# Column chunks of two thirds of the tokens moved beside the GLA stage, in a two-layer hybrid trunk

## The chip, the cores and the metric

The kernel runs on one core of one Trainium2 chip. The metric is the device time of one execution in microseconds. Before the change it is 2963.45 us, the median of three runs (2956.27 to 2968.64).

## The reference

The reference computes two layers over 256 context tokens and 2048 latent tokens of width 1024. Cut to what matters:

```python
def hybrid_layer(x, ctx, ...):
    h_l = rms_norm(x, norm_w) * (1.0 + scale_l) + shift_l      # adaLN; the same for ctx with its own scale and shift
    pl = split_proj(h_l @ w_in)                                # 3104 columns: a_*, b_*, c_*, d_*
    a_l, a_c = gla_mixer(pl, pc, ...)      # A: gated linear attention, both directions, in chunks
    b_l = fourier_mix(pl['b_v'], fnet_w)   # B: 2-D FFT over tokens and channels, then a matrix
    c_l, c_c = swa_mixer(pl, pc, ...)      # C: windowed attention, +-128 tokens and the context, RoPE, sink
    d_l, d_c = na_mixer(pl, pc, ...)       # D: neighbourhood attention on a 64-wide grid, 8 x 16, with bias
    y_l = concat([a_l * silu(pl['a_g']), b_l * silu(pl['b_g']),
                  c_l * silu(pl['c_g']), d_l * silu(pl['d_g'])]) @ w_out
    x = x + gate_l * y_l                   # the context likewise, in the first layer only
```

All of it is float32. The projections are done in three passes (high times high, high times low, low times high parts), so each product of a 256-token sub-block with a chunk of 256 columns is 2 × 8 × 3 = 48 matmuls of 128x128 by 128x256.

## The kernel before

**Tiling.** The tokens are nine sub-blocks of 256 (sub-block 0 is the context), in three groups: T1 = 0, 1, 2; T2 = 3, 4, 5; T3 = 6, 7, 8. The 3104 input columns are twelve chunks of 256 and one of 32: av, aqk, lr (for the GLA), bv (FNet), ckv, cq (window attention), dk, dv, dq (neighbourhood attention) and four gates ag, bg, cg, dg. `project` (line 277) does one chunk for one sub-block: its 48 matmuls (lines 220 to 222) and its eviction. A gate's eviction is a tanh on ACT (line 292), a product on DVE (line 293) and a store of 256 KB. cq, ckv, dq and dk pass `normrope` (line 367), a chain over ACT, DVE and POOL, then two or four transposes and stores. The weights of a chunk are loaded by `load_w` (line 204) in four pieces of 256 KB, each split into a high part (ACT, line 212) and a low part (line 213, by turns DVE and POOL). There are two buffers for high and low parts, three for raw ones.

**h.** `prep_h` (line 244) normalises a sub-block, applies the adaLN scale and shift and leaves a high and a low part (`hh`, `hl`, three buffers each, shared with `prep_mix` of the output projection). For T1 and T2 it also stores h to DRAM (line 261). `reload_h` (line 264) brings it back later, with one cast on ACT and one subtraction on DVE or POOL per half.

**Stages of one layer** (`trunk`, line 198). For T1 and for T2: `first_chunks` (prep_h, then av, lr, aqk); `mix_a`, whose GLA has bv, ckv, dk, dv (in T2 also dq) between its heads and its main part `gla_fast` (line 399). For T3: `first_chunks`, `mix_a`, and then bv, ckv, dk, dv. Then a guard on the GLA's range, `gla_bwd` (line 646), `fnet` (line 689), cq and dq of T3. Then `attention`: 144 items in layer 0 (64 of neighbourhood attention, 72 of window attention and 8 context rows), 128 in layer 1, in a software pipeline (line 876). Between its items stand the rest of the projections: the gates of T3, then h of T1 reloaded, cq, dq and the gates of T1, h of T2 reloaded, cq and the gates of T2, and the output projections `out_proj` (line 1088). An item is the scores on PE (line 830), one custom DVE step that adds the bias or mask and finds the minimum (line 836, two records each: the step and a read of its accumulator), exp on ACT (line 844), transposes on PE (line 862), and, for two items at a time, the product with v (line 922). The scores have one PSUM buffer. The bias of the neighbourhood items is loaded to one buffer for each of a pair's two items (line 1012). Four items of window attention make one block of 128 tokens; 16 neighbourhood items make one row group, `rg`.

**adaLN.** `ada` (line 114) computes shifts, scales and gates by products on DVE (line 167) with weights loaded in pieces of 256 KB. Part 0 of layer 1 (shift and scale, needed by layer 1's first `prep_h`) is in layer 0's T2; part 1 (the gate) of each layer is in its own T1.

**Order.** The Python text gives each instruction a priority, earlier ones first (blocks under `high_priority` go ahead). A planner replays the program on a model of the engines and sends to each engine's queue the first instruction that is ready there, provided its buffers are free. On the chip each queue runs in the order so written. Nearly all DMAs are issued on SP's queue.

## Time and profile before

| | |
|---|---|
| median of three runs | 2963.45 us |
| the profiled execution | 2951.03 us |
| its span | 2949.1 us |
| PE busy | 92% of the span |
| mean granted clock of PE | 0.959 |
| DVE, ACT, POOL busy | 55%, 36%, 28% |
| DMA | 458 MB, 155 GB/s in the mean |

The span runs from the first to the last instruction of the program. Stages by time: layer 0's GLA to about 600 us, gla_bwd and FNet to 770, attention to 1450; layer 1 begins at about 1480, its gla_bwd at about 2100, its attention at 2260, and it ends with output projections. A busy PE is not PE at its peak: the trace models the ends of matmuls, so the distance between starts tells the pace. The granted clock is 1.00 at 2.4 GHz and 0.50 at 1.2 GHz; a mean between them tells what share of the stretch was spent at each.

### The profile page before, as it was taken

The numbers are of one execution on the slowest core, as the hardware profiler recorded it, in microseconds if no ns is written. First come the engines' busy times: TensorE is split into PE (matmuls) and PEld (weight loads), VectorE is DVE, ScalarE is ACT, GpSimd is POOL, SyncE is SP. The second block draws the span as 40 slices with busy tenths as digits, with TensorE's granted clock in tenths as the row PEclk, the third lists the DMA queues.
The fourth block names the chain that finished last, engine by engine and source line by source line (L and its number), as shares of the span: only waits on it lengthen the run. The fifth ranks groups of instructions, "written<-read, shape, count | busy, mean of one in ns | idle before, by whom it ended". The sixth has DMA issues, their size and how long they took to land. (4 is left out here: it accounts for less than half of the span.)

```text
span 2949.1 us, 55777 instructions
## 1 busy us (share of the span) xinstructions
PE 2718.3 (92%) x21206; PEld 2410.2 (82%) x21206; DVE 1609.3 (55%) x3741; ACT 1070.9 (36%) x2344; POOL 837.3 (28%) x922
## 2 busy tenths in 40 slices
PE   5989988988999999999959889999879999999998
PEld 5889878976888778887859889889768888878788
DVE  7554775557355454645484553464483646455543
ACT  3333323322344343344224323334232444444432
POOL 3233222234132121312133332332351313121222
PEclk9999988999999999999979999989999999999999
DMA  8635544245565274554464664333465654456545
GB/s 273 194 108 163 169 136 126 84 145 166 162 192 167 81 215 129 158 157 124 147 193 134 196 185 144 93 111 104 119 190 162 199 164 135 146 163 190 161 149 180
DMA packets 476681, 458.00 MB, mean 155 GB/s; under 512 B 54763, under 2 KB 355565, under 8 KB 476013
## 3 DMA queue, kind: packets, MB, share of 16 engines
q1 hardware_dynamic: 472782, 440.66, 48.9%
q0 software_dynamic: 3616, 13.64, 1.9%
q8 instruction: 170, 2.79, 0.4%
q14 instruction: 113, 0.93, 0.1%
HBM read 339.56 MB, written 114.60 MB: 154 GB/s over the span
## 5 line engine op out<-in xcount | busy, mean ns | idle before, releaser
L220 PE MATMUL ps<-whi,hh 128*128 128x256 f32 x1968 | 586.4, 298 | 34.7 <-ACT hh L258 17.2
L222 PE MATMUL ps<-whi,hl 128*128 128x256 f32 x1968 | 582.0, 296 | 10.2 <-DVE hl L259 10.2
L221 PE MATMUL ps<-wlo,hh 128*128 128x256 f32 x1968 | 580.8, 295 | 6.4 <-PEq L639 6.4
L213 POOL TENSOR_TENSOR wlo<-wraw,whi 128x512 fp32r<-128x512 f32 x208 | 280.8, 1350 | 775.7 <-ACT whi L212 735.1
L220 PEld LDWEIGHTS ps<-whi,hh 128*128 128x128 f32 x1968 | 391.9, 199 | 46.4 <-ACT hh L258 19.0
L220 PE MATMUL ps<-hh,whi 128*128 128x256 f32 x1376 | 402.5, 292 | 5.3 <-ACT ev L311 2.3
L222 PEld LDWEIGHTS ps<-whi,hl 128*128 128x128 f32 x1968 | 391.3, 199 | 18.5 <-DVE hl L259 13.9
L221 PE MATMUL ps<-hl,whi 128*128 128x256 f32 x1376 | 403.3, 293 | 0.0
L222 PE MATMUL ps<-hh,wlo 128*128 128x256 f32 x1376 | 402.4, 292 | 0.0
L221 PEld LDWEIGHTS ps<-wlo,hh 128*128 128x128 f32 x1968 | 392.4, 199 | 11.0 <-issue 8.8
L212 ACT CAST whi<-wraw 128x512 fp32r<-128x512 f32 x416 | 242.3, 620 | 378.5 <-DMA wraw<-w_in 206.9
L844 ACT ACTIVATE S<-S,am 128x641 f32<-128x641 f32 (+5 forms) x272 | 226.1, 831 | 339.1 <-DVE am L836 324.5
L220 PE MATMUL pso<-mh,whi 128*128 128x256 f32 x1088 | 316.7, 291 | 5.3 <-DVE xo L1107 2.9
L222 PE MATMUL pso<-mh,wlo 128*128 128x256 f32 x1088 | 316.2, 291 | 2.3 <-POOL wlo L213 1.8
L221 PE MATMUL pso<-ml,whi 128*128 128x256 f32 x1088 | 315.1, 290 | 0.0
L213 DVE TENSOR_TENSOR wlo<-wraw,whi 128x512 fp32r<-128x512 f32 x208 | 187.9, 907 | 170.9 <-ACT whi L212 163.4
L220 PEld LDWEIGHTS ps<-hh,whi 128*128 128x128 f32 x1376 | 265.9, 193 | 15.2 <-issue 7.9
L222 PEld LDWEIGHTS ps<-hh,wlo 128*128 128x128 f32 x1376 | 265.8, 193 | 15.1 <-issue 14.8
L221 PEld LDWEIGHTS ps<-hl,whi 128*128 128x128 f32 x1376 | 266.0, 193 | 11.4 <-issue 11.0
L830 PE MATMUL pse<-kst,q 64*128 64x256 f32 (+2 forms) x1184 | 246.6, 457 | 13.6 <-DVE am L836 12.5
L191 POOL TENSOR_TENSOR rs<-ms,mhalf 128x8 f32<-128x8 f32 (+2 forms) x140 | 171.3, 1226 | 297.5 <-DVE ms L189 288.6
L862 PE MATMUL ppt<-idn,S 128*128 128x128 f32 x1360 | 243.6, 284 | 10.4 <-DVE pt L872 5.2
(203 smaller groups left out, 4866.4 us busy)
## 6 DMA issues: line engine op xcount, KB each, us to landing
wraw<-w_in SPq DMA_DIRECT2D x288, 256.0 KB
wraw<-w_out SPq DMA_DIRECT2D x128, 256.0 KB
adaw<-ada_w SPq DMA_DIRECT2D x82, 256.0 KB
scr_g<-ev SPq DMA_DIRECT2D x68, 256.0 KB
g<-scr_g SPq DMA_DIRECT2D x34, 512.0 KB
y<-scr_y SPq DMA_DIRECT2D x34, 512.0 KB
bias<-nbias SPq DMA_DIRECT2D x48, 256.0 KB
scr_h<-x SPq DMA_DIRECT2D x22, 512.0 KB
```

The source lines that it names most:

```text
L191: nc.gpsimd.tensor_tensor(out=rs, in0=ms, in1=self.mhalf.to_broadcast([128, n]), op=ALU.pow)
L212: nc.scalar.copy(hi[:, k], raw)
L213: (nc.gpsimd if i % 4 else nc.vector).tensor_tensor(out=lo[:, k], in0=raw, in1=hi[:, k], op=ALU.subtract)
L220: nc.tensor.matmul(out, ah(k), bh(k), start=(k == 0), stop=False)
L221: nc.tensor.matmul(out, ah(k), bl(k), start=False, stop=False)
L222: nc.tensor.matmul(out, al(k), bh(k), start=False, stop=(k == KB - 1))
L830: nc.tensor.matmul(p[:, lo:hi], q[r], k, start=True, stop=True, tile_position=(64 * o, 0))
L844: nc.scalar.activation(out=S[:, 0:w], in_=S[:, 0:w], func=AF.Exp, scale=-1.0, bias=m[:, 0:1], accum_out=m[:, 1:2])
L862: nc.tensor.transpose(p[:, i], S[:, (c0 + i) * 128:(c0 + i + 1) * 128], self.idn)
```

## The change

T1 and T2 get all their columns in `mix_a`: bv, ckv, dk, dv, cq, dq and the four gates, between the GLA's heads and its main part. T3 gets cq, dq and all gates in one call after `fnet`, ahead of the attention. The attention has no projections between its items but `out_proj`, and these are all of the kind that is issued behind an item. h is neither stored nor reloaded; `reload_h` goes. In layer 0, `out_proj` of T1 stands ahead of the last window blocks 4 to 9, where it stood behind them and behind the gates of T2. Part 0 of layer 1's adaLN moves from layer 0's T2 to its T3.

```diff
-    def prep_h(self, L, s, save, xs=None):
+    def prep_h(self, L, s, xs=None):
...
-            if save:
-                nc.sync.dma_start(self.sh[s][:, :, c], x)
-    def reload_h(self, s):
...
-                    run, nop = lambda f=ph[1]: f(), lambda *r: None
-                    items.append((None, run, nop) if ph[0] == "before" else (None, nop, lambda r, x, f=ph[1]: x == 2 and f()))
+                    items.append((None, lambda: None, lambda r, x, f=ph[1]: x == 2 and f()))
...
-            self.mix_a(L, T1, (0, [1]) if L == 0 else (1, [1]), lambda: self.chunks(L, T1, kv, h))
+            qs = ["dq", "cq"]
+
+            def rest(subs, h):
+
+                self.chunks(L, subs, kv + qs + gates[:2], h)
+                self.chunks(L, subs, gates[2:], h)
+            self.mix_a(L, T1, (L, [1]), lambda: rest(T1, h))
...
             h = self.first_chunks(L, T2, first)
-            self.mix_a(L, T2, (1, [0]) if L == 0 else None, lambda: self.chunks(L, T2, kv + ["dq"], h))
-            h = self.first_chunks(L, T3, first, False)
-            self.mix_a(L, T3)
+            self.mix_a(L, T2, None, lambda: rest(T2, h))
+            h = self.first_chunks(L, T3, first)
+            self.mix_a(L, T3, (1, [0]) if L == 0 else None)
             self.chunks(L, T3, kv, h)
-            ws = {nm: self.chunk_w(L, nm) for nm in ("cq", "dq")}
+            ws = {nm: self.chunk_w(L, nm) for nm in qs}
...
-            self.chunks(L, T3, ["cq", "dq"], h, ws)
-            hs = {}
-
-            def redo(subs, names):
-                with self.tc.high_priority():
-                    hs[subs[-1]] = {s: self.reload_h(s) for s in subs}
-                self.chunks(L, subs, names, hs[subs[-1]])
-            hs[8] = h
-            b, f = (lambda f, *a: ("before", lambda: f(*a))), (lambda f, *a: ("after", lambda: f(*a)))
-            gate = lambda subs: b(lambda: self.chunks(L, subs, gates, hs[subs[-1]]))
-            ctx = ([-2, -1], None) if L == 0 else ([], )
+            self.chunks(L, T3, qs + gates, h, ws)
+            f = lambda subs: ("after", lambda: self.out_proj(L, subs))
             T1 = lat(T1)
-            ph = [3, 2, [10, 11, 12, 13, 14, 15], gate(T3), b(redo, T1, ["cq", "dq"]), 0, ctx[0] + [0, 1, 2, 3], *ctx[1:], gate(T1)]
             if L == 0:
-                ph += [b(self.out_proj, L, T3), b(redo, T2, ["cq"]), 1, [4, 5, 6, 7, 8, 9], gate(T2), f(self.out_proj, L, T1)]
+                self.attention(L, 3, 2, [10, 11, 12, 13, 14, 15], 0, f(T3), [-2, -1, 0, 1, 2, 3], None, 1, f(T1), [4, 5, 6, 7, 8, 9])
             else:
-                ph += [b(redo, T2, ["cq"]), 1, [4, 5], [6, 7], [8, 9], gate(T2), b(self.out_proj, L, T3), f(self.out_proj, L, T1),
-                       f(self.out_proj, L, [3, 4]), f(self.out_proj, L, [5])]
-            self.attention(L, *ph)
+                self.attention(L, 3, 2, [10, 11, 12, 13, 14, 15], 0, f(T3), [0, 1, 2, 3], 1, [4, 5], [6, 7], [8, 9], f(T1), f([3, 4]), f([5]))
```

A number in the list of an attention is a row group of neighbourhood attention (16 items), a list of numbers is window blocks (4 items each), `None` is the context's rows, `f(...)` an output projection.

## Rows read from the trace of the kernel before

**Rows 1.** The page, part 1: busy us, share of the span, instructions.

```profile
PE 2718.3 (92%) x21206; PEld 2410.2 (82%) x21206; DVE 1609.3 (55%) x3741; ACT 1070.9 (36%) x2344; POOL 837.3 (28%) x922
```

**Rows 2.** Windows by stage: start:end length, each engine's busy us, clock, DMA share, GB/s.

```profile
50.00:100.00 50.00, 38.86 (x296) 37.73 (x297) 29.84 (x72) 16.37 (x27) 14.50 (x16) 1.00 0.45 133
100.00:300.00 200.00, 184.97 (x1384) 174.72 (x1382) 110.34 (x261) 72.40 (x156) 62.48 (x54) 0.94 0.51 161
300.00:500.00 200.00, 173.96 (x1186) 159.33 (x1185) 138.56 (x341) 64.78 (x141) 56.08 (x49) 0.85 0.46 141
500.00:600.00 100.00, 99.50 (x776) 92.55 (x775) 45.64 (x116) 42.37 (x105) 31.33 (x25) 1.00 0.32 108
600.00:770.00 170.00, 144.43 (x923) 127.12 (x922) 102.46 (x257) 42.56 (x93) 65.68 (x60) 0.93 0.52 154
770.00:1450.00 680.00, 663.51 (x5603) 555.13 (x5603) 355.62 (x848) 276.91 (x639) 153.99 (x234) 0.99 0.51 151
1450.00:1550.00 100.00, 67.67 (x485) 65.50 (x484) 70.91 (x158) 21.56 (x31) 29.32 (x28) 0.80 0.65 201
1550.00:1750.00 200.00, 186.97 (x1439) 178.86 (x1437) 96.02 (x179) 72.77 (x147) 68.75 (x54) 0.96 0.54 169
1750.00:1950.00 200.00, 180.06 (x1314) 168.18 (x1312) 96.35 (x212) 71.96 (x152) 64.06 (x59) 0.91 0.38 118
2100.00:2260.00 160.00, 132.41 (x849) 115.99 (x850) 99.39 (x246) 38.39 (x86) 60.43 (x52) 0.93 0.53 159
2260.00:2850.00 590.00, 580.29 (x4962) 479.82 (x4961) 322.62 (x753) 256.53 (x587) 144.61 (x220) 0.99 0.57 166
```

**Rows 3.** PE's waits in 300:500: total us, times, longest.

```profile
PE pk L430 <- DVE A L422: 7.8, 2, 4.3
...
PE ps L220 <- DVE nsq L376: 5.4, 2, 4.9
```

**Rows 4.** Timeline of PE in the second attention: start, us, instruction.

```profile
2403.54 0.28 PE L220 MATMUL ps<-hh,whi 128*128 128x256 f32 x1
2403.66 0.28 PE L221 MATMUL ps<-hl,whi 128*128 128x256 f32 x1
```

**Rows 5.** Groups of instructions by line: count | busy us, mean ns | idle before.

```profile
L273 POOL TENSOR_TENSOR hl<-x,hh 128x1024 fp32r<-128x1024 f32 x11 | 28.0, 2543 | 42.8 <-ACT hh L272 38.1 <-PE ppt L862 4.7
...
L213 DVE TENSOR_TENSOR wlo<-wraw,whi 128x512 fp32r<-128x512 f32 x208 | 187.9, 907 | 170.9 <-ACT whi L212 163.4 <-DVEq L639 6.2 <-DMA wck<-wck 0.3
...
L293 DVE SCALAR_TENSOR_TENSOR ev<-ev,ps 128x512 f32<-128x512 f32 x68 | 46.4, 683 | 43.5 <-ACT ev L292 43.3
```

**Rows 6.** Windows of line 292 (ACT, two), then of line 836 (DVE, two).

```profile
600.00:770.00 170.00, 3.58 (x6) 0.93 0.52 154
770.00:836.00 66.00, 3.54 (x6) 0.97 0.75 206
...
770.00:836.00 66.00, 10.78 (x26) 0.97 0.75 206
2300.00:2600.00 300.00, 60.02 (x138) 1.00 0.53 155
```

**Rows 7.** Windows of line 167 on DVE, 300:500.

```profile
300.00:500.00 200.00, 48.48 (x128) 0.85 0.46 141
```

**Rows 8.** Window of line 220 on PE; lines 221 and 222 count the same.

```profile
770.00:1450.00 680.00, 271.81 (x933) 0.99 0.51 151
```

**Rows 9.** Timeline of DVE, two window items in a row.

```profile
2815.01 0.86 DVE L836 CUSTOM_DVE_ANT_0 S<-pse,cmask,sink 128x640 f32<-128x640 f32 x1
...
2817.23 0.87 DVE L836 CUSTOM_DVE_ANT_0 S<-pse,cmask,sink 128x640 f32<-128x640 f32 x1
```

**Rows 10.** Timeline of SP's queue, a bias load.

```profile
1253.77 0.54 SPq L1012 DMA_DIRECT2D bias<-nbias  x1
```

**Rows 11.** Timeline of DVE, two pairs of neighbourhood items.

```profile
1251.66 0.95 DVE L836 CUSTOM_DVE_ANT_0 S<-pse,bias 128x768 f32<-128x768 f32 x1
...
1259.89 0.96 DVE L836 CUSTOM_DVE_ANT_0 S<-pse,bias 128x768 f32<-128x768 f32 x1 [1.11 <-DMA bias<-nbias]
```

More of the change, by code (lines that the diff above doesn't have):

```diff
@@ L259, in prep_h @@
             nc.vector.tensor_tensor(out=hl[:, :, c], in0=x, in1=hh[:, :, c], op=ALU.subtract)
-            if save:
-                nc.sync.dma_start(self.sh[s][:, :, c], x)
-        return hh, hl
-    def reload_h(self, s):
-        nc = self.nc
-        hh = self.hp.tile([128, KB, SUB], F32R, tag="hh", name="hh2")
-        hl = self.hp.tile([128, KB, SUB], F32R, tag="hl", name="hl2")
-        for t in range(2):
-            c = slice(t * 128, t * 128 + 128)
-            x = self.xp.tile([128, KB, 128], F32, tag="xa", name="x2", bufs=3)
-            nc.sync.dma_start(x, self.sh[s][:, :, c])
-            nc.scalar.copy(hh[:, :, c], x)
-            (nc.gpsimd if t else nc.vector).tensor_tensor(out=hl[:, :, c], in0=x, in1=hh[:, :, c], op=ALU.subtract)
         return hh, hl
@@ L1119, in scratch @@
             self.xdst[L] = [None] + [a["out"][s] for s in range(NSUB - 1)]
-        self.sh = sc("h", [128, KB, SUB])
         self.skq, self.sbv, self.sav = (sc(n, [128, 2, SUB]) for n in ("kq", "bv", "av"))
@@ L1155, in order, with first_chunks @@
                 + [(nm, s) for g in (subs[:n], subs[n:]) for nm in (c, d) for s in g])
-    def first_chunks(self, L, subs, names, save=True, xs={}):
+    def first_chunks(self, L, subs, names, xs={}):
         h = {}
@@ L1161, in first_chunks @@
             with self.tc.high_priority():
-                h[s] = self.prep_h(L, s, save and not (L == 1 and s == 0), xs.get(s))
+                h[s] = self.prep_h(L, s, xs.get(s))
             for nm in names:
```

## The prediction

> **What bounds the kernel now.** I first read the page's busy shares [rows 1]: PE (TensorE's matmuls) is busy 92% of the span, DVE 55%, so PE is the engine to follow, and only time in which PE stands or runs at the lower clock can be won. Then the windows by stage [rows 2]. For each stretch I add two losses: the idle time of PE, and (1 − granted clock) × length. A fall from 2.4 to 1.2 GHz shows as a mean below 1.00 and doubles PE's work while it lasts. For 300:500 that is 26.0 us idle + 0.15 × 200 = 30 us, so 56 us. In the same way: 27 us in 100:300, 0.5 in 500:600, 37 in 600:770, 23 in 770:1450 (the first attention, 680 us long), 52 in 1450:1550 (between the layers), 21 and 38 in 1550:1750 and 1750:1950, 39 in 2100:2260, 16 in 2260:2850 (the second attention). So the attention stretches, which hold nearly half of the time, lose 39 us together, and the GLA and FNet stretches with the layers' border lose some 270.
>
> Why does PE stand in the GLA stretches? The waits of 300:500 [rows 3] say: for DVE's A and for a projection's normalisation on DVE. These are chains of small steps at moments when no other matmuls are at hand. In the attention stretches there are always projections to fill with. One projection of one sub-block (256 tokens) by one column chunk is 48 matmuls, one every 0.12 us where PE is dense [rows 4], so 5.8 us.
>
> **Part by part.** The number of matmuls does not change; they move.
>
> *h kept out of DRAM.* 22 stores and 22 loads go, with 22 casts on ACT and 22 subtractions on DVE and POOL (28.0 us on POOL's eleven) [rows 5]. These stood beside an attention in which PE lost almost nothing, and no matmul wait among [rows 3] is for them. I take 0; at most it is a few microseconds in the two attentions.
>
> *The move.* Per layer, cq, dq and four gates of T1 (18 projections; 12 in layer 1, where sub-block 0 is skipped) and cq and four gates of T2 (15) go from the attention into the GLA stretches: 33 × 5.8 = 190 us and 27 × 5.8 = 155 us of PE time. The 12 gates of T3 go ahead of the attention as well, but by 770 six of them have already been evicted, and six more by 836 [rows 6]: the planner already pulls them forward, and they still move little. Each gate brings a DVE step of 0.68 us, each chunk two DVE splits of 0.91 us [rows 5], two POOL splits, four ACT casts, and four loads and a store on SP's queue. For layer 0's T1 and T2 that is 24 × 0.68 + 11 chunks × 1.8 = 36 us of DVE, and nine normalised q projections at no more than the 5.8 us of their own matmuls, 52 us. DVE has 151 us free in 100:500 [rows 2], and the stretch grows by about as much as is moved in. So these hide; without that cover PE would wait for PSUM in the way that [rows 3] shows for nsq (5.4 us there).
>
> What it wins in T1 and T2 of layer 0 (27 + 56 us): waits where filler was missing go, waits where PE's in-order queue has reached a step that DVE has not finished stay. Of 300:500 I keep the two waits for A (7.8) and as my choice 12 us for the next T's first chunk and the clock: 20 left, 36 won. Of 100:300 I keep 12 and win 15. Bounds: 0 and 83.
>
> In layer 1, 59 us in 1550:1950: by the same share (51 of 83, 61%) 36; I take 27, since out_proj already fills part of T1. Bounds 0 and 59. In the FNet stretches (37 and 39) the chain over DVE is long (DVE is busy 102 of 170 us) and only the gates that were not there already come in: 9 won in each; bounds 0 and 37.
>
> *The adaLN part.* 128 records of line 167 on DVE (64 products, 48.5 us) stand in 300:500 [rows 7], beside T2's GLA; they move to 500:600, where DVE is busy 45.6 of 100 us [rows 2]. That makes 94 of 100, so DVE nearly becomes T3's bound there; its 32 loads go along on SP. PE's projections of T3 cover most of it. I charge 8 us; bounds 0 and 30. The gain on the side of T2 is in the 36 above. What would be late next is gla_bwd, which follows the guard.
>
> *The border between the layers.* out_proj of T1 now stands ahead of the last 24 window items of layer 0 instead of behind everything. The first x of layer 1 is then ready while those items run, and prep_h no longer runs alone. Of 52 us I take 30 as won. Bounds: 0 and 45.
>
> *The attentions without filler.* This is the price. Paced with filler, 138 records of line 836 (two per item, so 69 items) take 300 us [rows 6]: 4.35 us per item. PE's own share of an item: in 770:1450 PE is busy 663.5 us [rows 2]; of these 3 × 933 filling matmuls [rows 8] at 0.12 take 336, and 327.5 over 144 items leaves 2.3 us. How fast an item goes bare is not shown over any length. Single pairs show it: two window items 2.22 us apart [rows 9]. For neighbourhood items the bias tile has one buffer. Its load is issued only after its reader ended, at 1253.77 [rows 10], and the first item of the next pair starts at 1259.89 instead, held by the DMA, 8.23 us after the first of the pair before [rows 11]. So a neighbourhood item costs between 2.3 (PE) and 4.1 us; three of four pairs change the bias. I take 3.3 us for these, which is near the middle, and 2.5 us for window items, near their row. Bare are: in layer 0 items 13 (13 are done by 836 [rows 6]) to 59, when T3's out_proj can fill, and 14 more between T3's out_proj running out and T1's becoming ready; in layer 1, taken alike, some 44. That is together 104 items: 42 neighbourhood × 1.0 + 62 window × 0.2 = 54 us, and 6 us of lower clock: 60. Bounds: 0 and 4.35 − 2.3, times 104: 213.
>
> Sum: −15 − 36 + 8 − 9 − 30 − 27 − 9 + 60 = **−58 us**. The profiled execution took 2951.0 us by the clock (span 2949.1); the median shown is 12 us above that. 2951 − 58 + 12 = **2905 us**.
>
> **Rivals.**
> *The bare attention keeps its pace* (slower). If its items stay at 4.35 us, because the planned order of queues and loads holds them and not the filler, the price is 213 instead of 60: 2905 + 153 = 3058. For it: the pace is the same in stretches with different fillers, and bias loads already hold single items. Against it: 2.22 us [rows 9]. It decides from 118 of savings / 104 items, so from 3.4 us per bare item.
>
> *PE's clock falls in the bare attention* (slower). PE's 2.3 us become 4.6: 104 × 2.3 = 239 instead of 60, so 3084. Against it: in 50:100 PE is busy only 38.9 of 50 us, with gaps, and the clock is 1.00 [rows 2]. For it: 300:500 with PE busy 87% has 0.85. With filler the attention's clock was 0.99; no long bare stretch exists. The Trainium skill (TensorE: Matmul & The Clock Gate, "Why this matters for your kernels") warns that pauses between bursts of matmuls put the clock back to half. By that rule the bias waits of bare items would bring this rival about; the trace agrees so far as its falls stand in stretches with idle time.
>
> *The GLA waits stay.* If nearly all are in-order waits for DVE, filler behind the waiting instruction cannot pass. Then only the border's 30 are won against 60 + 8: 2963 + 38 = 3001. For it: the waits in [rows 3] name DVE. Against it: 500:600, with GLA and projections at hand, loses 0.5.
>
> *All of it fills.* The GLA, FNet and border losses fall from 270 to 40 together, the price of 60 stays: 2963 − 230 + 60 = 2793. Against it: the first steps of each T wait for chains that no filler shortens.
>
> *The change does little*, because the planner places work by readiness and moves it already: 2963. For it: T3's gates. Against it: T1's wait for h to come back from DRAM and cannot be pulled.
>
> **How the numbers follow.** Forecast 0.45 (its own range 2870 to 2945), all filled 0.12, pace kept 0.15, GLA waits stay 0.15, clock falls 0.06, little change 0.07. A measurement here tells 0.5% (15 us) from no change. Faster: 0.43 of the forecast, all of the second, 0.02 of the fourth: 0.57. Same: 0.02 of the forecast, 0.05 of the last, 0.06 of the fourth: 0.13. Slower: 0.30. The range from 2800 to 3040 leaves out half of the two outer cases on either side.
>
> **What would show it.** Right: PE idle and clock losses of the GLA windows (as many projections later) cut by more than half; layer 1's first prep_h beside window items; line 836 at 2.5 to 3.3 us per item early in each attention; PE's filling matmuls in the attentions only out_proj's. Wrong: bare items at over 3.4 us, waits for the bias DMA of tens of microseconds, a clock under 0.95 there, or waits for A and nsq in the GLA stretches as before; a gla_bwd that starts late behind the adaLN part.

## The result and the profile after

The changed kernel takes 2983.95 us (median; 2981.3 to 2985.7) beside 2962.65 for the kernel before in the same session: a ratio of 1.0071, 95% interval 1.0049 to 1.0094. It is 21 us slower where 58 less were forecast. The profiled execution took 2983.05 us, its span is 2981.2, 32 longer than before.

First the page's busy shares of the kernel after:

```profile
PE 2719.0 (91%) x21206; PEld 2395.4 (80%) x21206; DVE 1598.8 (54%) x3730; ACT 1045.8 (35%) x2322; POOL 810.7 (27%) x911
```

PE is busy for the same 2719 us as in [rows 1], so no work was added; it stands longer. The windows by stage of the kernel after say where (start:end, length, busy us of PE, PEld, DVE, ACT, POOL, granted clock, DMA share, GB/s):

```profile
100.00:766.00 666.00, 646.82 (x5099) 620.82 (x5099) 368.73 (x834) 230.03 (x496) 204.00 (x165) 0.98 0.42 133
766.00:946.00 180.00, 155.74 (x1031) 137.97 (x1032) 106.77 (x261) 43.62 (x96) 72.69 (x61) 0.95 0.59 176
946.00:1429.00 483.00, 431.59 (x3497) 329.10 (x3496) 250.89 (x638) 187.99 (x461) 82.11 (x168) 0.95 0.52 151
1429.00:1540.00 111.00, 107.11 (x887) 88.44 (x888) 69.88 (x174) 49.40 (x111) 29.34 (x53) 0.95 0.33 102
1540.00:2226.00 686.00, 647.70 (x5090) 620.82 (x5088) 341.35 (x723) 239.83 (x498) 222.32 (x179) 0.98 0.43 135
2226.00:2411.00 185.00, 158.34 (x1039) 139.83 (x1039) 103.66 (x251) 41.87 (x92) 66.08 (x57) 0.91 0.57 167
2411.00:2910.00 499.00, 443.35 (x3638) 334.37 (x3638) 266.11 (x651) 204.96 (x493) 85.78 (x179) 0.94 0.52 151
```

Read them as [rows 2] were read: length minus busy, and (1 − clock) × length. The GLA of layer 0 (100:766) loses 19 + 13 us. The border (1429:1540) loses 9 where [rows 2] lost 52. But the two attentions (946:1429 and 2411:2910) lose 51 + 24 and 56 + 30, where [rows 2] lost 23 and 16.

From here on the losses of four stages are compared, with the stage limits taken from each trace itself: the GLA of layer 0 ends 10 us ahead of gla_bwd's first sum, an attention begins 5 us ahead of its first item, and that of layer 0 ends where layer 1's first prep_h begins. "Loss" is PE's idle time plus half of the time in which the lower clock was granted. Times are medians; the ratio is to the kernel before, timed beside it in the same session. Between sessions the kernel before moved by 6 us (2957 to 2963), so runs of different sessions are compared by their ratios, of which 0.001 is 3 us. Two of these stages, in the kernel before:

```profile
769.00:1491.00 722.00, 688.91 (x5803) 579.89 (x5801) 381.75 (x904) 284.51 (x650) 166.96 (x247) 0.98 0.52 156
1491.00:2101.00 610.00, 559.41 (x4210) 529.57 (x4210) 306.66 (x658) 215.73 (x449) 193.10 (x166) 0.94 0.45 139
```

The first holds part of what [rows 2] counts to the border, so attention 0 stands at 44 in the table and not at 23.

| kernel | time, us | ratio [95%] | GLA 0 | attention 0 | border and GLA 1 | attention 1 |
|---|---|---|---|---|---|---|
| before | 2957 to 2963 | 1 | 87 | 44 | 89 | 13 |
| after | 2984.0 | 1.0071 [1.0049, 1.0094] | 34 | 80 | 56 | 85 |
| e8 T1 all, T2 all but gates | 2996.1 | 1.0124 [1.0098, 1.0150] | 73 | 68 | 84 | 55 |
| e9 T2's part alone | 2931.5 | 0.9901 [0.9884, 0.9917] | 53 | 41 | 60 | 68 |
| e10 T1's part alone | 2980.8 | 1.0074 [1.0050, 1.0098] | 65 | 59 | 100 | 40 |
| e13 T2's part, layer 0 alone | 2919.0 | 0.9869 [0.9842, 0.9897] | 54 | 48 | 68 | 13 |
| e14 the same, border order of after | 2928.9 | 0.9905 [0.9881, 0.9929] | 49 | 57 | 70 | 14 |
| e15 whole change, layer 0 alone | 2938.0 | 0.9935 [0.9914, 0.9956] | 30 | 92 | 88 | 9 |
| e16 whole change, layer 1 alone | 3001.1 | 1.0147 [1.0122, 1.0171] | 86 | 50 | 64 | 81 |

gla_bwd with FNet loses 33 and 38 us before, 34 and 42 after, and the tail behind the last item 4 less than before. The losses grow by 23 in all from before to after; the other 9 of the span's 32 must be looser packing inside what counts as busy.

Inside the attentions of the kernel after, by windows (columns as above):

```profile
946.00:1057.00 111.00, 97.73 (x853) 65.27 (x852) 67.06 (x179) 57.22 (x144) 16.35 (x41) 0.97 0.65 180
1057.00:1160.00 103.00, 88.81 (x664) 63.90 (x665) 55.19 (x135) 39.73 (x97) 17.04 (x36) 0.90 0.43 123
1160.00:1226.00 66.00, 66.00 (x560) 58.90 (x558) 25.99 (x65) 17.28 (x42) 9.40 (x15) 1.00 0.56 169
1226.00:1302.00 76.00, 66.12 (x490) 40.35 (x488) 47.51 (x149) 34.98 (x104) 13.93 (x46) 0.93 0.38 108
1302.00:1371.00 69.00, 57.75 (x473) 47.30 (x474) 34.50 (x78) 27.47 (x56) 10.61 (x15) 0.93 0.61 169
...
2411.00:2525.00 114.00, 97.20 (x837) 64.80 (x837) 68.16 (x180) 57.31 (x145) 16.67 (x41) 0.93 0.61 174
2525.00:2625.00 100.00, 87.04 (x659) 62.43 (x660) 54.20 (x132) 39.47 (x97) 17.06 (x36) 0.91 0.44 126
2625.00:2693.00 68.00, 67.19 (x575) 59.77 (x573) 28.09 (x69) 19.34 (x48) 10.86 (x19) 1.00 0.59 173
2693.00:2910.00 217.00, 191.92 (x1569) 147.37 (x1569) 115.66 (x274) 88.83 (x207) 41.20 (x84) 0.94 0.49 142
```

and of the items' step on DVE alone (line 822 in the kernel after, 836 before; two records per item as in [rows 6]):

```profile
946.00:1057.00 111.00, 35.87 (x80) 0.97 0.65 180
1057.00:1160.00 103.00, 21.28 (x51) 0.90 0.43 123
1160.00:1226.00 66.00, 7.43 (x21) 1.00 0.56 169
1226.00:1302.00 76.00, 22.46 (x65) 0.93 0.38 108
1302.00:1371.00 69.00, 13.86 (x30) 0.93 0.61 169
...
2411.00:2525.00 114.00, 35.87 (x80) 0.93 0.61 174
2525.00:2625.00 100.00, 21.11 (x50) 0.91 0.44 126
...
2693.00:2910.00 217.00, 47.03 (x104) 0.94 0.49 142
```

Three kinds of stretches alternate. Bare ones (946:1057, 1226:1302, 2411:2525) pass 112 items and lose 57 us, 0.5 per item; an item takes 111 / 40 = 2.8 us in the first. In 1160:1226 and 2625:2693 `out_proj` fills everything, 21 items pass and less than 1 us is lost. In the others (1057:1160, 1302:1371, 2525:2625, 2693:2910) out_proj and items stand side by side: 117 items, and 100 us lost, 0.86 per item, more than without it. What runs there on PE beside the items, from the groups of 2525:2625:

```profile
L220 PE MATMUL pso<-mh,whi 128*128 128x256 f32 x66 | 20.3, 311 | 0.2 <-ACT mh L1070 0.2
```

196 matmuls (three such groups) in 100 us, and PE's waits in the second attention of the kernel after (total us, times, longest):

```profile
PE ppt L848 <- DVE pt L858: 26.9, 10, 4.6
PE pse L816 <- DVE am L822: 24.2, 31, 8.7
```

The second is an item's score buffer, still being read by the step of the item before; the first is a copy on DVE that comes late, up to 4.6 us, because DVE is held by something else. That something was my first suspect.

### The profile page after: what moved, and what is told of

Same layout as the page of the kernel before. It is cut to its first block, busy times and chain, and to the rows that moved or that the text cites. A ratio compares the mean times of both kernels' runs of the same rounds, so it can differ in the third digit from the quotient of the medians.

```text
span 2981.2 us, 55854 instructions
## 1 busy us (share of the span) xinstructions
PE 2719.0 (91%) x21206; PEld 2395.4 (80%) x21206; DVE 1598.8 (54%) x3730; ACT 1045.8 (35%) x2322; POOL 810.7 (27%) x911
## 5 line engine op out<-in xcount | busy, mean ns | idle before, releaser
L220 PE MATMUL ps<-whi,hh 128*128 128x256 f32 x1968 | 580.4, 295 | 22.0 <-DVE nsq L362 16.5
L222 PE MATMUL ps<-whi,hl 128*128 128x256 f32 x1968 | 573.5, 291 | 4.8 <-DVE hl L259 4.8
L213 POOL TENSOR_TENSOR wlo<-wraw,whi 128x512 fp32r<-128x512 f32 x208 | 288.8, 1388 | 882.0 <-ACT whi L212 852.0
L221 PE MATMUL ps<-hl,whi 128*128 128x256 f32 x1376 | 395.5, 287 | 0.0
L213 DVE TENSOR_TENSOR wlo<-wraw,whi 128x512 fp32r<-128x512 f32 x208 | 196.9, 952 | 211.5 <-ACT whi L212 203.9
L816 PE MATMUL pse<-kst,q 64*128 64x256 f32 (+2 forms) x1184 | 256.5, 476 | 52.9 <-DVE am L822 50.6
L848 PE MATMUL ppt<-idn,S 128*128 128x128 f32 x1360 | 235.3, 294 | 51.7 <-DVE pt L858 40.8
L848 PEld LDWEIGHTS ppt<-idn,S 128*128 128x128 f32 x1360 | 153.0, 145 | 149.8 <-DVE pt L858 43.9
```

The costliest lines, as they stand in the source:

```text
L213: (nc.gpsimd if i % 4 else nc.vector).tensor_tensor(out=lo[:, k], in0=raw, in1=hi[:, k], op=ALU.subtract)
L220: nc.tensor.matmul(out, ah(k), bh(k), start=(k == 0), stop=False)
L221: nc.tensor.matmul(out, ah(k), bl(k), start=False, stop=False)
L222: nc.tensor.matmul(out, al(k), bh(k), start=False, stop=(k == KB - 1))
L816: nc.tensor.matmul(p[:, lo:hi], q[r], k, start=True, stop=True, tile_position=(64 * o, 0))
L848: nc.tensor.transpose(p[:, i], S[:, (c0 + i) * 128:(c0 + i + 1) * 128], self.idn)
```

## The experiments

### Is it DVE's wait for y?

Ahead of out_proj, `prep_mix` multiplies y by the gate on DVE, and DVE, in order, waits for y from DRAM. DVE's waits at that product in the second attention, of the kernel before and of the kernel after:

```profile
DVE y L1083 <- DMA y<-scr_y: 38.7, 12, 5.1
```

```profile
DVE y L1069 <- DMA y<-scr_y: 28.8, 12, 4.5
```

They were there before, but with projections beside them. How such a wait reaches PE, from the timelines of DVE (two lines) and PE (one) in the kernel after; in brackets, the idle time of the engine just before:

```profile
1310.87 1.23 DVE L1069 TENSOR_TENSOR y<-y,g 128x1024 f32<-128x1024 f32 x1 [5.07 <-DMA y<-scr_y]
1312.08 0.94 DVE L822 CUSTOM_DVE_ANT_0 S<-pse,bias 128x768 f32<-128x768 f32 x1
1313.08 0.93 PE L816 MATMUL pse<-kst,q 64*128 64x384 f32 x6 [3.60 <-DVE am L822]
```

In the four stretches with out_proj and items side by side, DVE waits 62 us for y, and PE waits 62 of its 64 idle us for a copy or an item's step on DVE. In the three bare stretches DVE waits only 9 us for y; PE's wait there is mostly for the items' own step (28 of 40 idle us).

Theory A: the waits for y have lost their cover. Theory B: the bare items' own chain sets the price. Theory C: out_proj comes in solid bursts and leaves the other items bare.

**A second buffer for y**, in the kernel after (e1) and before (e2):

```diff
-            y = self.xp.tile([128, KB, 128], F32, tag="xb", name="y", bufs=1)
+            y = self.xp.tile([128, KB, 128], F32, tag="xb", name="y", bufs=2)
```

(the same for `sq` in the norm, which shares the tag).

> The changed kernel with two buffers instead of one for y in the output projection's preparation (and for the square in norm_x, which shares them). Theory A: the surplus of the attentions' cost is that DVE stands in order before the product y*g until y has landed (74 us of DVE waits for scr_y in the two attentions), which the projections on PE had covered and nothing covers now; it expects 2925 to 2950 against 2984, DVE's waits for scr_y more than halved, and PE's waits for pt and am in the stretches with output projections (13 us in 1057:1160) nearly gone. Theory B: the bare items' own chain (scores, minimum, bias load) is the cost; it expects 2974 to 2990. Theory C: the output projections run in solid bursts ahead of the items and leave the items bare; it expects 2970 to 2990 too.

> The kernel before with the same second buffer, as a control. Theory A: the waits of DVE for y lie beside projections on PE there, so shortening them wins little: 2950 to 2965 against 2963. Theories B and C expect no change either; a gain as large as in the changed kernel would speak against A.

Measured: 2994.5 us (1.0113 [1.0086, 1.0140]) and 2977.0 (1.0065 [1.0043, 1.0087]). By the ratios both got slower, by 12 and 19 us. The second buffer didn't take the wait away; in the second attention of e1:

```profile
DVE y L1069 <- DMA y<-scr_y: 35.4, 14, 5.7
```

So nothing follows on A, and both times lie above all that the theories expected. Why the buffer costs time isn't settled; in e2 the GLA of layer 0 loses 96 instead of 87, and the border with layer 1's GLA 101 instead of 89.

**The product on GpSimd** (e5):

```diff
-            nc.vector.tensor_tensor(out=y, in0=y, in1=g, op=ALU.mult)
+            nc.gpsimd.tensor_tensor(out=y, in0=y, in1=g, op=ALU.mult)
```

> The changed kernel with one edit: the product y*g ahead of an out_proj runs on GpSimd instead of VectorE (12 products of 128x1024 in the attention of layer 0, 10 or more in that of layer 1, in the trace of after each behind a wait of 2 to 5 us for y). So no instruction of VectorE waits for y from DRAM any more; the chain of the attention items is as it was. Theory A (in the changed kernel VectorE, in order, stands at y while TensorE has nothing else to do: about 44 us of the idle TensorE in the two attentions are the products and these waits): the waits for y on VectorE go to zero and the time falls by 25 to 45 us, to 2935-2960. Theory B (the items' own chain of waits sets the pace when nothing runs beside them): VectorE's waits go, TensorE's idle time in the attentions stays within 10 us of the 110, time 2975-2985. Theory C (out_proj goes in solid bursts and leaves the items bare): as B. Against all: rd and the sink column run on GpSimd too, and stand behind the product: if they become the wait, the time grows by 5 to 20 us.

Measured: 2995.95 us (1.0142 [1.0112, 1.0172]). DVE's wait for y is gone, and another has come, as the last sentence of the expectation feared. PE's waits in the second attention of e5:

```profile
PE ppt L852 <- POOL rd L851: 23.3, 7, 4.7
PE pse L816 <- DVE am L822: 22.2, 31, 8.3
```

GpSimd's small copies `rd` for the items now stand behind the product. The gain of 25 to 45 us that A expected did not come, but the run exchanged one wait for another and settles little.

**No product at all** (e11 in the kernel after, e12 in the kernel before). y goes by DMA straight into both operands of out_proj; the gate, its load and the split are left out:

```diff
-            nc.sync.dma_start(y, self.y[L][s][:, :, c])
-            nc.sync.dma_start(g, self.sg[L][s][:, :, c])
-            nc.vector.tensor_tensor(out=y, in0=y, in1=g, op=ALU.mult)
-            nc.scalar.copy(hh[:, :, c], y)
-            (nc.gpsimd if t else nc.vector).tensor_tensor(out=hl[:, :, c], in0=y, in1=hh[:, :, c], op=ALU.subtract)
+            nc.gpsimd.dma_start(hh[:, :, c], self.y[L][s][:, :, c])
+            nc.gpsimd.dma_start(hl[:, :, c], self.y[L][s][:, :, c])
```

> The changed kernel without the work ahead of out_proj: y is loaded straight into both operands of out_proj by GpSimd's DMA queue. Left out are the product with the gate, the gate's load, and the split in a high and a low part, so VectorE, ScalarE and GpSimd do nothing for y, and VectorE never stands at it. TensorE's matmuls are the same. Theory A (VectorE's products and their waits for y hold the bare items; some 44 us of TensorE's idle time): TensorE's idle time in the two attentions falls from 110 to about 65 us, the time by 35 to 60 us against the changed kernel, and clearly less in the same edit of the kernel before (0 to 15), where projections cover them. Theory B (the bare items' own chain): idle stays within 15 us of 110, the time falls by as little as in the kernel before.

> The kernel before with the same edit (y straight into out_proj's operands, without gate and split). In its attentions TensorE stands only some 43 us in all, and projections are at hand while VectorE makes or awaits the product. Theory A: 0 to 15 us less than before, 2945-2960, so the difference between the two kernels turns from +25 to about -10 to -30. Theory B: both change alike, and the difference between the kernels stays at 15 to 30 us.

Measured: 2948.7 us (0.9954 [0.9938, 0.9971]) and 2913.2 (0.9842 [0.9825, 0.9858]). Leaving out the work for y wins 35 us in the kernel after and 45 in the kernel before, where A expected 0 to 15. Without it the distance between the two is 35 us instead of 21. Windows of the two attentions of e11:

```profile
939.00:1436.00 497.00, 443.22 (x3532) 339.02 (x3530) 242.51 (x633) 180.67 (x458) 92.98 (x192) 0.92 0.64 153
2400.00:2882.00 482.00, 438.04 (x3668) 334.61 (x3666) 244.64 (x631) 190.32 (x479) 95.10 (x202) 0.96 0.66 157
```

They still lose 54 + 40 and 44 + 19 us. So DVE's work for y is not what sets the two kernels apart. But the run exchanged waits as e5 did. PE's waits in the second attention of e11:

```profile
PE pso L220 <- DMA mh<-scr_y: 13.4, 7, 3.8
PE ppt L848 <- DVE pt L858: 0.4, 1, 0.4
```

PE's waits for the late copy, 41 us in the two attentions of the kernel after, are all but gone, and 29 us of waits for the loads of y have come. That y lands late and nothing covers it is therefore not excluded as a part of the price.

### Is it the place of a single part?

In the kernel after: T3's gates back between the items, behind window blocks 10 to 15 (e3); T3's out_proj placed later (e4); out_proj of T3 and of layer 0's T1 cut into its four column groups and spread over the items (e6); T1's out_proj of layer 0 back behind the last items (e7).

```diff
+            g3 = ("after", lambda: self.chunks(L, T3, gates, h))              # e3
-                self.attention(L, 3, 2, [10, 11, 12, 13, 14, 15], 0, f(T3), [-2, -1, 0, 1, 2, 3], None, 1, f(T1), [4, 5, 6, 7, 8, 9])
+ e3             self.attention(L, 3, 2, [10, 11, 12, 13, 14, 15], g3, 0, f(T3), ...)
+ e4             self.attention(L, 3, 2, [10, 11, 12, 13, 14, 15], 0, [-2, -1, 0, 1, 2, 3], None, 1, f(T3), f(T1), [4, 5, 6, 7, 8, 9])
+ e6             self.attention(..., 0, f(T3, 0), [-2, -1, 0], f(T3, 1), [1, 2], f(T3, 2), [3], None, f(T3, 3), 1, f(T1, 0), [4], f(T1, 1), ...)
+ e7             self.attention(..., 0, f(T3), [-2, -1, 0, 1, 2, 3], None, 1, [4, 5, 6, 7, 8, 9], f(T1))
```

> The changed kernel with one part undone: the four gates of T3 stand behind the window blocks 10 to 15 in the attention again and not ahead of it, so that they can fill the first items. Theory B: these 69 us per layer cover the 40 first items, which lose 33 us together in both layers now: 2945 to 2960. Theory A: the gates are used up before the output projection's y is waited for, so only the early items' part is won: 2960 to 2975. Theory C: 2955 to 2975.

> The changed kernel with T3's output projection behind the other items in the text (behind row group 1 in layer 0, behind the window blocks in layer 1), so that it may only fill. Theory C: no solid bursts (18 evictions of the output projection without an item between), the items keep a filler longer: 2945 to 2970. Theory A: the waits for y stay and lie beside other items: 2975 to 2995. Theory B: 2970 to 2990.

> The changed kernel with T3's out_proj in both layers, and T1's in layer 0, cut into their four column groups, which are placed one after the other between the attention items (T3's over [-2..3] and the context rows in layer 0, over [0..3] and row group 1 in layer 1; T1's over [4..9]). The same instructions, the same products y*g at the start. Theory C (bursts leave the items before and after them bare): TensorE's idle time in the attentions falls from 110 us to 70 or below, the time to 2935-2960. Theory A (waits for y): the waits stand where they were at the start of each out_proj, but with less beside them there: time 2975-2995. Theory B (chain of bare items): filler spread over more items covers more of them: each column group is 144 matmuls at 0.12 us, some 17 us of TensorE's work, so 2950-2975.

> The changed kernel with one part undone: T1's out_proj of layer 0 stands behind the last attention items again, as in the kernel before, so that layer 1's first steps cannot begin beside those items. In the comparison of the stages the border gave back about 43 us (idle and clock, 52 to 9). If that gain belongs to the order of T1's out_proj: the time grows by 25 to 45 us, to 3010-3030. Rival: the border gains because of what is no longer there (T2's gates behind it), whatever the order: the time stays at 2980-2990. In either case the attention of layer 0 has 10 to 25 us more bare items in the middle and the same at its end.

Measured: e3 2976.6 (1.0064 [1.0044, 1.0084]), e4 2975.4 (1.0065 [1.0041, 1.0088]), e6 2979.25 (1.0080 [1.0051, 1.0109]), e7 2974.6 (1.0054 [1.0027, 1.0081]). The changed kernel's own ratio is 1.0071, so by the ratios these are 5 us below it to 3 above, and none can be told from it: each interval holds 1.0071. None is near the 25 to 40 that a cause would be worth. Spreading out_proj took 10 us off the idle time of the two attentions (99 instead of 110) and lost 7 more to the clock, so theory C is a small part at most. And e7 says that the border's gain does not belong to the order of T1's out_proj: undoing it costs nothing. In e7 layer 1's first prep_h begins at 1461 us, before the last item at 1473: the planner sends T1's out_proj ahead by itself, once T2's gates no longer stand before it.

### Which tokens?

A mixture of the two kernels (e8) has T1 as after, T2 as after but for its four gates, T3 as before:

```diff
-            self.mix_a(L, T1, (0, [1]) if L == 0 else (1, [1]), lambda: self.chunks(L, T1, kv, h))
+            self.mix_a(L, T1, (L, [1]), lambda: rest(T1, h))
-            self.mix_a(L, T2, (1, [0]) if L == 0 else None, lambda: self.chunks(L, T2, kv + ["dq"], h))
+            self.mix_a(L, T2, None, lambda: self.chunks(L, T2, kv + qs, h))
...
+            ph = [3, 2, [10, 11, 12, 13, 14, 15], gate(T3), b(redo, T2, []), 0, gate(T2)]
```

> Between the two kernels: T1 has all its column chunks beside its GLA (as after), T2 all but its four gates (bv, ckv, dk, dv, dq, cq beside its GLA), and T3 as before. T3's and T2's gates stay between the attention items, T2's h is stored and loaded again for that; adaLN's part and the order at the border are as after. So GLA of T1 and the border keep the changed kernel's gain, GLA of T2 part of it, and 24 of the 54 projections that stood beside the attention in each layer of the kernel before stay there. Theory A+B (what was lost is cover of the items, whichever wait stands there): attentions lose 50-70 us less than in the changed kernel, GLA of T2 some 20 us more: 2905-2945, below both kernels. Rival (as with T3's gates alone put back, which gave 2977: the loss sits at the out_proj, which the gates do not cover): 2960-2985.

Measured: 2996.1 us, slower than both; both theories' bounds are missed. (By the code the kernel before has 45 projections there in layer 0, not the 54 of the expectation: 12 gates of T3, 18 of T1, 15 of T2.) The table shows a GLA of layer 0 that wins 14 us only, and attentions that lose 66 more. The changed kernel, whose GLA wins 53, differs there by T2's gates, so these seemed to win the most. That led to the parts alone, in the kernel before:

```diff
-            self.mix_a(L, T2, (1, [0]) if L == 0 else None, lambda: self.chunks(L, T2, kv + ["dq"], h))
+            self.mix_a(L, T2, None, lambda: self.chunks(L, T2, kv + ["dq", "cq"] + gates, h))                                  # e9
...
-            self.mix_a(L, T1, (0, [1]) if L == 0 else (1, [1]), lambda: self.chunks(L, T1, kv, h))
+            self.mix_a(L, T1, (0, [1]) if L == 0 else (1, [1]), lambda: self.chunks(L, T1, kv + ["dq", "cq"] + gates, h))      # e10
```

(in e9 adaLN's part goes on to T3, and the steps that redid these chunks between the items go, each in its run).

> The kernel before with T2's part of the change alone: T2 gets all its chunks beside its GLA (cq and the four gates as well), its h is not stored, and adaLN's part of layer 1 goes on to T3. T1 and T3 stay as before, with T1's cq, dq and gates and T3's gates between the attention items; T1's out_proj at the end of layer 0 as before. The run that moved T1's chunks and left T2's gates (2996, 37 above before) and the changed kernel (25 above) differ by T2's gates. Theory D (filler helps a stage only up to what its chains leave idle; T2's GLA had the large loss, T1's the small one, and the attention needs about as much as T1 and T3 bring): T2's GLA wins 35 to 40 in layer 0 and some 25 in layer 1, the attentions lose 10 to 40 in all, time 2915-2945, below both kernels. Theory E (each filler that is moved out of an attention costs there what it wins beside the GLA, whichever it is): 2955-2980.

> The kernel before with T1's part of the change alone: T1 gets cq, dq and its gates beside its GLA, its h is not stored; T2 and T3 as before, with T2's cq and gates between the attention items. Theory D: T1's GLA wins 10 to 20 us in layer 0 and 0 to 10 in layer 1 (its out_proj of T2 fills there already), the attentions lose 30 to 60 in all, since the items between T3's gates and T2's are left bare: time 2970-3000. Theory E: 2955-2980. With the run of T2's part alone the two should make up the changed kernel's difference of 25 to within 20 if the parts add; if both alone are slower than, or both equal to, the kernel before by more than that, they don't add.

Measured: 2931.5 us (0.9901) and 2980.8 (1.0074). T2's part wins 27, T1's part loses 22, both in theory D's ranges of time; e10 lies only 1 us above E's. In the GLA of layer 0 T2's part wins 34 and T1's 22; but the attentions lose 52 more in e9, not 10 to 40. The sum of the parts is −5, and the whole change is +21: by the measure of the expectation (to within 20) the parts don't add. What is in neither part is small where it was tried: putting T3's gates back wins 2 us (e3) and undoing the order at the border 5 (e7), neither told from nothing. That both parts take filler from the same items is the explanation left; no run shows it alone.

### Which layer?

e9 still loses 68 us in layer 1's attention. So each part went into one layer alone: T2's part into layer 0 (e13), the same with T1's out_proj ahead of the last items (e14), the whole change into layer 0 (e15) and into layer 1 (e16):

```diff
         for L in range(2):
+            way = ('t2', 'before')[L]          # e13; e14: ('t2o', 'before'); e15: ('after', 'before'); e16: ('before', 'after')
+            t1all, t2all = way == "after", way != "before"
```

> T2's part of the change in layer 0 alone (all of T2's chunks beside its GLA, its h not stored, adaLN's part on to T3); layer 1 is that of the kernel before. In the run with T2's part in both layers (2931), layer 1's attention lost 68 us where the kernel before lost 13, and its GLA from 1500 on lost 61 where the kernel before lost 62. Theory F (layer 1's GLA was already filled by layer 0's out_proj, so what is moved there only strips its attention): 2931 - 55 = 2876, range 2865-2895. Theory G (the stage sums mislead, and what one stage wins the next loses): 2925-2950.

> As the run before it (T2's part in layer 0 alone), and T1's out_proj of layer 0 ahead of the last 24 window items, as in the changed kernel. With T2's gates gone from the end of layer 0, T1's out_proj already ran beside the last items in the run with T2's part alone (layer 1's first prep_h at 1436, last item at 1470), so nothing is left at the border for the order to win: theory F 2865-2895, within 10 us of the run before it. Rival: an earlier x for layer 1 lets more of its GLA start beside the items: 15 to 30 us less than the run before it.

> The whole change in layer 0 alone; layer 1 is that of the kernel before. By the stages: layer 1's attention loses 13 instead of 85 (72 less than the changed kernel), its GLA from 1550 on 62 instead of 52 (10 more), FNet and tail nothing. Theory F: 2984 - 62 = 2922, range 2905-2935, so faster than the kernel before. Theory G: 2950-2985.

> The whole change in layer 1 alone; layer 0 is that of the kernel before. Theory F: 2963 + 72 - 10 = 3025, range 3010-3040. If the layers add, this run's and the last run's differences from the kernel before make up the 21 to 25 us of the change. Theory G: 2970-3000.

Measured against 2958.65: e13 2919.0 (−40), e14 2928.9 (−30), e15 2938.0 (−21), e16 3001.1 (+42). −21 + 42 = 21: the layers add, and the net loss is layer 1's, while layer 0 as a whole wins. The sizes lie between theories F and G: the stage sums have the signs right and are too large. e13 is 43 us above F's value and 24 above its range, though its second attention is as full as it was before. Windows of the second attention of e13, then of e16:

```profile
2227.00:2799.00 572.00, 562.22 (x4792) 462.26 (x4791) 315.83 (x741) 251.66 (x575) 139.86 (x212) 0.99 0.58 167
```

```profile
2421.00:2921.00 500.00, 447.34 (x3687) 337.29 (x3688) 267.17 (x653) 205.80 (x496) 85.85 (x179) 0.94 0.53 151
```

In e15 the border is closed, and yet border and GLA of layer 1 together lose 88, as before (89). Windows of e15, its border and the GLA behind it, then of that GLA in the kernel before:

```profile
1439.00:1540.00 101.00, 99.44 (x829) 82.42 (x830) 63.42 (x162) 45.16 (x103) 25.48 (x48) 0.97 0.39 119
1540.00:2096.00 556.00, 510.91 (x3809) 482.57 (x3807) 283.53 (x624) 195.68 (x418) 174.54 (x145) 0.93 0.45 140
```

```profile
1550.00:2101.00 551.00, 516.14 (x3921) 487.83 (x3919) 261.88 (x556) 201.77 (x429) 175.75 (x149) 0.95 0.43 135
```

The GLA behind the closed border loses 45 + 39 instead of 35 + 28. In e13, with the same layer 1, 21 us of the two together are won. What makes this difference is not settled.

### Is the price missing filler?

Four transposes of idn by idn behind each item's scores, into a PSUM bank that nothing reads, in the kernel after (e17) and before (e18):

```diff
+        z = self.ph.tile([128, 512], F32, tag="h", name="fill")
+        for i in range(4):
+            nc.tensor.transpose(z[:, i * 128:i * 128 + 128], self.idn, self.idn)
```

> The changed kernel with four more transposes of 128x128 per attention item (271 items in the two layers, idn by idn, into a PSUM bank that nobody reads), right behind the item's score matmuls: useless work that depends on nothing. At 0.12 to 0.16 us each (transposes of the items in dense stretches) that is 130 to 174 us of TensorE's time. Theory B (a bare item leaves TensorE about 0.6 us free, and nearly all items of the changed kernel are bare; filler takes this time): TensorE's idle time and clock loss in the attentions (165 us) fall by 80 or more, and the time grows by only 30 to 90 us, to 3015-3075. Rival (the waits stand in TensorE's own order, filler only comes on top): the time grows by all of it, to 3110-3155.

> The kernel before with the same filler, 130 to 174 us. Its attentions lose 57 us of idle time and clock in all, so there is little to take: the time grows by 100 to 170 us, to 3060-3130. Theory B: it grows by 60 to 110 us more than the changed kernel does, so that the changed kernel with filler is the faster of the two by 40 to 90 us. Rival: both grow alike, and the changed kernel stays 15 to 30 us behind.

Measured: 3044.6 us (1.0299 [1.0263, 1.0335]) and 3079.7 (1.0425 [1.0386, 1.0463]). The same useless work (4 × 272 items) costs the kernel before 123 us and the kernel after 61 (67 by the ratios), and with it the changed kernel is the faster one, by 35 us. Windows of the attentions of e17, then of e18:

```profile
944.00:1459.00 515.00, 487.75 (x4076) 386.08 (x4076) 258.36 (x649) 194.46 (x469) 86.39 (x173) 0.97 0.51 145
2434.00:2964.00 530.00, 494.70 (x4172) 387.46 (x4174) 266.66 (x652) 208.02 (x495) 86.18 (x179) 0.96 0.51 143
...
762.00:1548.00 786.00, 753.06 (x6372) 642.82 (x6371) 397.80 (x945) 289.00 (x656) 164.37 (x246) 0.99 0.50 145
2311.00:2886.00 575.00, 560.91 (x4848) 464.21 (x4846) 293.71 (x706) 240.97 (x556) 118.32 (x201) 0.99 0.50 141
```

and PE's waits in the second attention of e17:

```profile
PE pse L816 <- DVE am L825: 12.5, 8, 7.3
PE ppt L851 <- DVE pt L861: 12.1, 5, 5.8
```

The losses of the changed kernel's attentions fall from 165 to 98 us (a fall of 80 or more was expected), both kinds of wait to about half, and the granted clock rises from 0.95 and 0.94 to 0.97 and 0.96. In the kernel before there was nothing to take: its two attentions lose 57 us without the useless work and some 61 with it. The difference in growth, 56 to 62 us, is at or just below the lower end of the 60 to 110 expected; the lead of 35 us is a little below the 40 to 90. Much of the time lost beside the items is thus free time that any matmul takes: what the change took away there is cover. This does not choose between A and B, since either wait can be covered so; the stretches say that the bare items' own chain stands in the one kind and DVE's waits for y in the other. The scores' single PSUM buffer, on which the bare items wait, was not doubled in any run. Of the attentions' 108 us of growth, filler gave back 67; the rest is not settled.

## Why the prediction was wrong

**The failed step is the price of the attentions.** It gave 60 us; the two attentions lose 36 + 72 = 108 more than before. The price per bare item was about right: 54 + 6 over 104 items is 0.58, and the bare stretches lose 0.5 each. For neighbourhood items 3.3 us were taken, and 946:1057 shows 2.8, without any stretch of bias waits. What failed is the count: "when T3's out_proj can fill", and after it T1's, the items were taken as covered. out_proj covers the few that pass in its solid bursts (21). Of the others 229 lose time, where 104 were counted, and the 117 that stand beside out_proj lose more (0.86) than the bare ones: there DVE, which the items need, waits for out_proj's y. In layer 0, where 60 items were counted, 112 pay; in layer 1 it is 117 instead of 44. Layer 0 pays its 36 us out of what its GLA wins; layer 1 does not earn its 72, and the whole change in it alone is +42.

**GLA of layer 0: right.** −15 − 36 + 8 = −43 forecast, −53 measured. The adaLN part left no loss that the stages show; alone it wasn't tried. For T1's and T2's shares 15 and 36 were chosen; the parts alone win 22 (e10) and 34 (e9).

**Border −30 and layer 1's GLA −27: half.** Together they gave 33 of 57. In e16, without the border, the GLA of layer 1 wins 25, as forecast. The border's own 43 are real (9 beside the 52 of [rows 2]), but they don't add to the rest: in e15 they are lost again in layer 1's GLA, in e13 21 us of them remain. The sum counted the border and the GLA behind it as two separate losses; why they don't add is not settled. Nor is it the order of T1's out_proj that wins them (e7, and e14 is 10 us slower than e13).

**FNet −18: wrong.** 33 and 38 us of loss became 34 and 42. In layer 0 the stage grew by as much as PE's work in it, T3's gates among it: 151 us with 128 busy became 181 with 156.

**h kept out of DRAM: 0** was taken. Nothing in the runs speaks against it; it wasn't tried alone.

With the measured terms the sum is −53 + 5 − 33 + 108 − 4 (tail) = +23, and with the 9 of packing +32, the growth of the span.

**The rivals.** None of them happened as such. The pace of 4.35 us per item was not kept (2.8 in the bare stretch 946:1057). The clock fell as that rival said, but to a mean of 0.90 to 0.97, so at 1.2 GHz for at most a fifth of a stretch and not for all of it: 55 us of the 165 in the attentions. Here the Trainium skill (TensorE: Matmul & The Clock Gate, "Why this matters for your kernels") bears on it: it warns that pauses between bursts of matmuls put the clock back. The trace agrees in direction, since 0.95 and 0.94 became 0.97 and 0.96 when useless transposes closed pauses. What was held against this rival, a clock of 1.00 in 50:100 in spite of gaps, was misread. The trace has no record of the granted clock before 66.0, and a window reads 1.00 where there is none. All but 1.4 of the 11 idle us lie before 62. From 62 to 66 the matmuls of a projection start 0.21 to 0.22 us apart, and 0.12 behind that. From PE's timeline in the kernel before:

```profile
63.20 0.41 PE L221 MATMUL ps<-wlo,hh 128*128 128x256 f32 x1
63.42 0.41 PE L222 MATMUL ps<-whi,hl 128*128 128x256 f32 x1
...
67.69 0.28 PE L221 MATMUL ps<-wlo,hh 128*128 128x256 f32 x1
67.81 0.28 PE L222 MATMUL ps<-whi,hl 128*128 128x256 f32 x1
```

So from 62 to 66, behind the gaps, PE ran at the pace of the lower level, and the row does not speak against the rival.

**The signs that were named.** PE's losses in layer 0's GLA cut by more than half: seen. Layer 1's first prep_h beside window items: seen (42 records of the items' step lie in 1429:1530). 2.5 to 3.3 us per bare item: seen (2.8). A clock under 0.95 in the attention, named as a sign of failure: seen (0.90 to 0.94 in all stretches but one that lose time). What I did not name is the sign that mattered, idle time where out_proj and items stand together.

**What beats both kernels** is T2's part in layer 0 alone: 2919.0 us, 0.9869 [0.9842, 0.9897]. There the GLA that stood most [rows 2] gets its filler, 33 us won, the attention, which keeps T1's and T3's, loses only 4 more than before, and 21 come from the border and layer 1's GLA.

## What to carry to other kernels

Filler that any stage can use is a stock: before moving it, read how much each item or step of the stage that gives it away needs (here 0.5 us of PE per item), and leave that. Don't count other work in that stage as cover unless the trace shows it: beside out_proj, which brought waits of its own, the items lost 0.86, and spreading it over them (e6) did not help. And try a move of several parts one part and one layer at a time: here the whole change was −21 us in layer 0 and +42 in layer 1, hidden in a +21, and one part in one layer was −40.

## What was not expected of the hardware

Useless matmuls can be half free: 1088 transposes that cost the full kernel 123 us (0.113 each) cost the one with bare items 61 to 67. The granted clock was 0.90 and 0.91 in 1057:1160 and 2525:2625, where PE was busy 89 of 103 and 87 of 100 us. The means hide short stays at 1.2 GHz behind single waits. One came right behind the wait of 3.60 us at 1309.5 that is shown above:

```profile
1314.20:1317.60 3.40, 3.40 (x16) 3.00 (x16) 1.65 (x5) 1.29 (x3) 1.65 (x2) 0.50 0.99 293
```

Another, from 1232.3, came behind waits of only 1.15 and 0.44 us. Over the whole span the clock hardly moved: 0.959 before, 0.963 after, 0.968 with the useless transposes.
